# An encoder block in exact halves: eight seven-product columns instead of five, and low halves formed by an adding DMA queue

## The chip, the cores and the metric

The kernel runs on one core of a Trainium2 chip. The core has a matrix engine (TensorE, PE in the profile), a vector engine (VectorE, DVE), a scalar engine (ScalarE, ACT), a general engine (GpSimd, POOL) and a queue engine (SyncE, SP). Each runs its own list of instructions in order; they wait for one another by semaphores. PE reads its operands from SBUF, the on-chip memory of 128 partitions, and adds its products up in PSUM, eight banks of 128 x 512 float32; DVE and ACT read PSUM. DMA transfers are issued from SP, ACT or POOL and are carried by 16 DMA engines. The metric is the time of one execution in microseconds (us), measured on the device.

## What is computed

One layer of a residual block on x, 512 tokens by 1024 features, all in float32:

```python
h = rms_norm(x, g1)
x = x + (sigmoid(g_A) * y_A + sigmoid(g_B) * y_B) @ w_out      # two attention branches of h
x = x + conv_glu(rms_norm(x, g2))

def conv_glu(h):
    hid = h @ w_up                          # 1024 -> 2 * 2816
    hid = causal depthwise conv of width 3 along the tokens, + bias
    gate, up = hid[:, :2816], hid[:, 2816:]
    return (silu(gate) * up) @ w_down       # 2816 -> 1024
```

The change touches only conv_glu, the last 45% of the time.

## The kernel before

**Halves.** PE's fast format keeps only part of a float32. Each operand is therefore split: the high half is the value rounded to that format (a cast on ACT), the low half is the value minus the high half (a subtraction on DVE). A product is three matmuls: high x high, high x low, low x high (mm3, L251). Whatever is multiplied must first pass through ACT and DVE for this.

**Up-projection.** The 2 x 2816 columns of w_up are worked off as 22 column pairs, j = 0 to 21, each 128 gate columns and the 128 up columns that belong to them ("column j" below). A column's weights are 1 MB; SP loads them two columns ahead into two raw buffers, ACT and DVE split them one column ahead (split_gen, L204). A plain column (up_body, L935) is 2 x 8 products of 128 x 128 weights with 512 tokens: 48 matmuls of 512 columns. Columns 0 and 1 run interleaved with the end of the stage before.

A column in SEVEN (L63) is computed by seven block products instead of eight (up_seven, L986). Weights and the normed tokens are cut into 2 x 2 blocks (halves of the features; gate and up columns, or halves of the tokens), and by Winograd's form of Strassen's scheme seven products of blocks or of block sums give all four result blocks. This is 7 x 4 x 3 = 84 matmuls of 256 columns. It needs sums of token blocks (ts, four tiles, formed once at the start of the stage), sums of weight blocks (block_sums, L173, four DVE instructions, in the column pair before last) and halves of seven blocks instead of four (split_seven, L188), and the result blocks are put together by four copies on ACT and five additions on DVE (L1003 to L1024). Before, SEVEN is columns 5, 8, 11, 14 and 17.

After a column's products come the convolution (conv, L849: one ACT and two DVE instructions for the gate, the same for the up part), SiLU on ACT and the gating product on DVE (L928). The result u of column j lies in one of four slots of ub.

**Pairs.** The down-projection uses the seven-product scheme as well, on pairs of columns. When columns 2i and 2i+1 are done, pair_sums(i) forms the block sums (L898 to L901, in a tile st with one buffer, and in u itself) and the halves of seven operands: four go to a tile ax of 2048 columns, three to a tile ay of 1536 (L904 to L912; the first half of each tile holds the high halves, the second the low ones). The high half is written by ACT (L908), the low half by DVE (L909). For i = 0 to 8 this happens in the up-projection, pairs 9 and 10 are finished inside the down-projection.

**Down-projection.** Two passes over the 11 pairs. The first (s = 0) takes the four products that use ax, the second (s = 1) the three that use ay. A step of a pass, dn0_i or dn1_i, is 24 or 18 matmuls of 512 columns. Its weights come from SP into the same raw buffers and are split on ACT and DVE one step ahead (split_down, L139). Split n = 1 is placed behind the last column's convolution (L155 to L158).

**Where the operands lie.** ax0 to ax7 have eight buffers of the tag "ax"; ax8 takes a buffer of the token sums, whose last use is column 17. All ay up to pair 6 share one buffer: each is stored to DRAM (L933) on POOL's queue and fetched again (fetch, L948) into space that has come free. fetch 0 to 4 stand in the program behind column 18, 5 and 6 in the first pass (L1175). keep[0] is a place for weights that the second pass needs again.

**Order.** The program gives the instructions in the order of the code. The order in which each engine gets them is laid out at compile time by a list scheduler along a modelled timeline, so that an instruction that is ready by the model can be taken ahead of earlier ones that are not. In the profile the work on a pair runs up to 20 us behind the end of its columns, and fetches appear ahead of their place in the code.

Of the kernel before, what the change touches and what calls it, by code (L numbers as in the profile page):

```python
# [8 lines left out]
F32 = mybir.dt.float32  # L9
F32R = mybir.dt.float32r  # L10
AF = mybir.ActivationFunctionType
ALU = mybir.AluOpType
# [3 lines left out]
P = 128  # L16
S = 512
# [42 lines left out]

CHUNKS = _chunks()

SEVEN = (5, 8, 11, 14, 17)  # L63


@with_exitstack
def block_kernel(ctx: ExitStack, tc: tile.TileContext, x, xt, params, g2, rbx, wts, wd0, wd1, out):
    nc = tc.nc
    V, A, G, PE, SP = nc.vector, nc.scalar, nc.gpsimd, nc.tensor, nc.sync
# [41 lines left out]
    keep = {}  # L111
# [58 lines left out]
    def is_seven(i):  # L170
        return i < len(order) and order[i] in [f"up{j}" for j in SEVEN]

# [69 lines left out]
    def run_chunk(key, body, pieces=4):  # L242

        sp = split_gen(pos[key] + 1, pieces)
        for _ in body(*splits.pop(key)):
            next(sp, None)
            yield
        for _ in sp:
            pass
# [12 lines left out]
    pp = ctx.enter_context(tc.tile_pool(name="pp", bufs=1, space=PSUM))  # L262
    dram = ctx.enter_context(tc.tile_pool(name="dram", bufs=1, space=bass.MemoryType.DRAM))
    htd = dram.tile([NT, 2, P, S], F32, tag="htd", name="htd")
    ayd = dram.tile([7, P, 1536], F32, tag="ayd", name="ayd")


    reset = pool_c.tile([P, S], F32, tag="reset", name="reset")
# [560 lines left out]
    hi, lo = splits.pop("wo3")  # L829
# [8 lines left out]
    fp = late["pool"] = ctx.enter_context(tc.tile_pool(name="fp", bufs=1))  # L838
# [5 lines left out]
    pairs = {}  # L844
# [4 lines left out]
    def conv(ps, tile_idx, c):  # L849
        cw = lambda j: par[:, C_CW + 2 * NF * j + tile_idx:C_CW + 2 * NF * j + tile_idx + 1]  # L850
        tap = A.activation(c, ps, AF.Identity, scale=cw(2), bias=par[:, C_CB + tile_idx:C_CB + tile_idx + 1])
        late["tap"] = (tap,)
        V.scalar_tensor_tensor(c[:, 1:], ps[:, 0:S - 1], cw(1), c[:, 1:], op0=ALU.mult, op1=ALU.add)
        V.scalar_tensor_tensor(c[:, 2:], ps[:, 0:S - 2], cw(0), c[:, 2:], op0=ALU.mult, op1=ALU.add)
# [9 lines left out]
    def gate(j, pg):  # L864
        g = fp.tile([P, S], F32, tag="cg", name=f"cg{j}", bufs=1)
        conv(pg, j, g)
        A.activation(g, g, AF.Silu)
        return g

    def pair_sums(i):  # L870

        u0, u1 = ub[:, 2 * i % 4, :], ub[:, 2 * i % 4 + 1, :]
        u = ub[:, 2 * i % 4:2 * i % 4 + 2, :].rearrange("p a b -> p (a b)")
        lo_, hi_ = slice(0, 256), slice(256, 512)
        t = {}
        if i < 8:
            ax = fp.tile([P, 2048], F32R, tag="ax", name=f"ax{i}", bufs=8)
            ay = fp.tile([P, 1536], F32R, tag="ay", name=f"ay{i}")
        elif i == 8:

            ax = fp.tile([P, 2048], F32R, tag="ts", name=f"ax{i}", bufs=4)
            ay = fp.tile([P, 1600], F32R, tag="wxh", name=f"ay{i}")[:, 0:1536]
            keep[0] = fp.tile([P, S], F32, tag="hg", name="t2_0")
        else:

            ax = late["hp"].tile([P, 2048], F32R, tag=f"ax{i}", name=f"ax{i}")
            ay = late["hp"].tile([P, 1536], F32R, tag=f"ay{i}", name=f"ay{i}")
        pairs[i] = (ax, ay)

        def sums():  # L890
            t["st"] = st = fp.tile([P, 768], F32, tag="st", name=f"st{i}", bufs=1)
            s1, s42 = st[:, 0:256], st[:, 256:768]
            if i == 9:

                s42 = fp.tile([P, S], F32, tag="cg", name="s42_9", bufs=1)
            s4, s2 = s42[:, 0:256], s42[:, 256:512]
            t["s42"] = s42
            ins = [V.tensor_tensor(s1, u0[:, hi_], u1[:, hi_], op=ALU.add),  # L898
                   V.tensor_tensor(u0[:, hi_], u0[:, lo_], u0[:, hi_], op=ALU.subtract),
                   V.tensor_tensor(s2, s1, u0[:, lo_], op=ALU.subtract),  # L900
                   V.tensor_tensor(s4, u1[:, lo_], s2, op=ALU.subtract)]  # L901
            return ins

        def halves(a, parts):  # L904
            ins, n = [], a.shape[-1] // 2
            for o, src in parts:
                sl = slice(o, o + src.shape[-1])
                A.copy(a[:, sl], src)  # L908
                ins.append(V.tensor_tensor(a[:, n + o:n + sl.stop], src, a[:, sl].bitcast(F32), op=ALU.subtract))  # L909
            return ins  # L910
        return (sums, lambda: halves(ax, ((0, u[:, 0:768]), (768, t["st"][:, 0:256]))),
                lambda: halves(ay, ((0, u[:, 768:1024]), (256, t["s42"]))))  # L912

    def keep_place(i):
# [8 lines left out]
    def up_fin(j, pg, pu, g=None):  # L923
        if g is None:
            g = gate(j, pg)
        u = ub[:, j % 4, :]
        conv(pu, NF + j, u)
        late["fin"] = (V.tensor_tensor(u, g, u, op=ALU.mult),)  # L928
        if j % 2 == 1 and j // 2 < 9:
            for step in pair_sums(j // 2):  # L930
                step()
            if j // 2 < 7:
                G.dma_start(ayd[j // 2], pairs[j // 2][1].bitcast(F32))  # L933

    def up_body(j):  # L935
        def body(hi, lo):
            pg, pu = BANK(f"pg{j}", j - 1), BANK(f"pu{j}", j - 1)
            yield from up_mm(pg, hi, lo, 0, 0, S)
            g = gate(j, pg)
            if j in (2, 3):  # L940
                next(late["ts"])
            yield from up_mm(pu, hi, lo, P, 0, S)
            up_fin(j, pg, pu, g)
            if j in (2, 3):
                next(late["ts"])
        return body

    def fetch(i):  # L948

        tag = {0: "sx", 1: "wxl"}.get(i, "ts" if i < 5 else "ax")  # L950
        n, bufs = {"sx": (1536, 1), "wxl": (1600, 1), "ts": (2048, 4), "ax": (2048, 8)}[tag]
        ay = fp.tile([P, n], F32R, tag=tag, name=f"ay{i}", bufs=bufs)[:, 0:1536]
        G.dma_start(ay, ayd[i])
        pairs[i] = (pairs[i][0], ay)
# [3 lines left out]
    ts = {}  # L958
# [27 lines left out]
    def up_seven(j):  # L986
        def body(hi, lo, wh, wl):
# [35 lines left out]
            V.tensor_tensor(hu[:, left], b7, hu[:, right], op=ALU.add)  # L1023
            V.tensor_tensor(hu[:, right], hu[:, right], pc[:, 1], op=ALU.add)  # L1024
            up_fin(j, None, hu, g)
            yield
        return body
# [4 lines left out]
    def up_first(j):  # L1032
        def body(hi, lo):
            pg, pu = BANK(f"pg{j}", 0), BANK(f"pu{j}", 0)
            halves.append((hi, lo, pg, pu))
            yield from up_mm(pg, hi, lo, 0, 0, 256)
            yield from up_mm(pu, hi, lo, P, 0, 256)
            if j == 1:
                n = 0
                for i, (h, l, g, u) in enumerate(halves):  # L1040
                    for o, ps in ((0, g), (P, u)):
                        for _ in up_mm(ps, h, l, o, 256, S):
                            n += 1
                            if n == 1 or 4 <= n < 8:
                                next(late["ts"])
                            yield
                    up_fin(i, g, u)
        return body

    late["ts"] = token_sums()  # L1050
    for j in range(NF):
        body = up_first(j) if j < 2 else up_seven(j) if j in SEVEN else up_body(j)
        for _ in run_chunk(f"up{j}", body, pieces=4 if j < 2 else 2):
            pass
        if j == 18:
            for i in range(5):
                fetch(i)


# [48 lines left out]
    def late_pair(steps):  # L1108

        for step in steps:  # L1110
            for ins in step():
                chain("halves", ins)
            yield
# [34 lines left out]
    def down_body(s, i):  # L1148
        order_ = ((1, 2, 5, 7), (6, 3, 4))[s]

        def body(hi, lo):
            for n, p in enumerate(order_):
                product(s, p, i, hi, lo)
                if s == 0 and i == NP - 1:
                    fin0(p)
                if n == 2:
                    next(steps, None)
                yield
        return body
# [10 lines left out]
    def steps0():  # L1170
        yield
        for i in (9, 10):
            ss[i] = pair_sums(i)
            yield from late_pair(ss[i][:2])
            fetch(i - 4)  # L1175

    def steps1():
        tmp["x"] = [fp.tile([P, 2, D], F32, tag="ax", name=f"x_{r}", bufs=8) for r in range(2)]
# [7 lines left out]
    for s in range(2):  # L1186
        steps = (steps0, steps1)[s]()
        for i in range(NP - 2 * s):
            for _ in run_chunk(f"dn{s}_{i}", down_body(s, i), pieces=2):
                pass  # L1190

    for _ in split_gen(pos[f"dn1_{NP - 1}"], 2):
        pass
# [13 lines left out]
def _layout(inputs):  # L1207
# [12 lines left out]
    for i, (key, kn, parts) in enumerate(CHUNKS[:-2 * NP]):  # L1220
        views = [f[name][0][r0:r0 + kn * P, c0:c0 + n] for name, r0, c0, n in parts]
        w = views[0] if len(views) == 1 else np.concatenate(views, axis=1)
        if key in [f"up{j}" for j in SEVEN]:

# [26 lines left out]
```

## Time and profile before

| | us |
|---|---|
| median of 3 runs | 726.53 (726.07 to 726.63) |
| profiled execution | 726.66 |
| its span, first to last instruction | 724.9 |
| PE busy in the span | 718.6 (99%) |
| DVE busy | 565.4 (78%) |
| ACT busy | 401.5 (55%) |
| POOL busy | 53.6 (7%) |
| up-projection, column 2 to the first matmul of the down-projection | 402.8 to 615.6 |

The profile is of one execution. A row of a group of instructions gives the line of the code, the engine, the operation, out<-in by the program's names, the shape and count, then busy time in us and the mean of one in ns, then the idle time of the engine before them with what ended it. Rows of waits give total, count and longest. Rows of the timeline give start and duration. The instructions of an engine overlap a little, so durations add up to somewhat more than busy time.

### The profile page before, as it was taken

How to read it: one execution, taken by the hardware profiler on the slowest of the kernel's cores; microseconds unless marked ns; L12 is line 12 of the kernel's file. 1: busy time of each engine (PE TensorE's matmuls, PEld its weight loads, DVE VectorE, ACT ScalarE, POOL GpSimd, SP SyncE). 2: the span in 40 equal slices, each digit the busy share in tenths (PEclk: the TensorE clock that was granted, in tenths of full speed). 3: DMA queues.
4: the chain of work that ended last, by engine and by line, in shares of the span. 5: the costliest groups of instructions: out<-in, count | busy, mean ns of one | idle time of the engine just before them, and what ended most of it. 6: DMA issues, size and time to landing. Idle time of an engine off the chain costs nothing.

```text
span 724.9 us, 10589 instructions
## 1 busy us (share of the span) xinstructions
PE 718.6 (99%) x4019; PEld 627.5 (87%) x4019; DVE 565.4 (78%) x1030; ACT 401.5 (55%) x727; POOL 53.6 (7%) x95
## 2 busy tenths in 40 slices
PE   8999999999999999999999999999999999999997
PEld 8999998888988888888889889889898988888886
DVE  6678867775988888566275799998979985997686
ACT  6675656657767676442254556655545653543541
POOL 2701200000101011000012000000000100000000
PEclk9999999999999999999999999999999999999999
DMA  8632232211313111314536613544335553564563
GB/s 308 250 131 78 83 117 74 74 59 58 118 63 113 59 59 59 136 68 144 195 149 239 203 62 156 186 135 160 118 145 186 181 184 117 173 243 174 177 222 116
DMA packets 24786, 100.91 MB, mean 139 GB/s; under 512 B 2592, under 2 KB 7328, under 8 KB 17184
## 3 DMA queue, kind: packets, MB, share of 16 engines
q1 hardware_dynamic: 21792, 87.00, 33.8%
q0 software_dynamic: 2656, 13.11, 5.0%
q8 instruction: 31, 0.51, 0.3%
q14 instruction: 19, 0.16, 0.1%
q10 hardware_dynamic: 288, 0.14, 0.1%
HBM read 88.44 MB, written 11.80 MB: 138 GB/s over the span
## 4 chain that ended last, share of the span: by engine, by line
PE 98%; DMA 1%; SPq 0%; DVE 0%; ACT 0%; DVEq 0%; issue 0%
PE P L1087 14%; PE p L998 7%; PE pg L254 4%; PE pg L253 4%; PE pg L255 4%; PE pu L254 4%; PE pu L255 4%; PE pu L253 4%; PE qkB L255 2%; PE gB L255 2%; PE qkB L253 2%; PE gA L253 2%; PE gA L254 2%; PE gB L253 2%; PE gA L255 2%; PE qkB L254 2%
## 5 line engine op out<-in xcount | busy, mean ns | idle before, releaser
L253 PE MATMUL pg<-hth,whi_up 128*128 128x512 f32 (+1 forms) x152 | 55.7, 367 | 0.0
L255 PE MATMUL pg<-hth,wlo_up 128*128 128x512 f32 (+1 forms) x152 | 55.7, 366 | 0.0
L254 PE MATMUL pg<-htl,whi_up 128*128 128x512 f32 (+1 forms) x152 | 55.7, 366 | 0.0
L254 PE MATMUL pu<-htl,whi_up 128*128 128x512 f32 (+1 forms) x152 | 55.6, 366 | 0.0
L253 PE MATMUL pu<-hth,whi_up 128*128 128x512 f32 (+1 forms) x152 | 55.6, 366 | 0.0
L255 PE MATMUL pu<-hth,wlo_up 128*128 128x512 f32 (+1 forms) x152 | 55.6, 365 | 0.0
L1087 PE MATMUL P<-whi_dn,ax 128*128 128x512 f32 x176 | 54.4, 389 | 0.0
L149 ACT CAST whi_dn<-raw_dn 128x1024 fp32r<-128x1024 f32 x33 | 34.3, 1051 | 25.5 <-PE P L1087 15.2
L145 DVE TENSOR_TENSOR wlo_dn<-raw_dn,whi_dn 128x1024 fp32r<-128x1024 f32 x33 | 40.0, 1224 | 9.2 <-ACT whi_dn L149 9.1
L228 DVE TENSOR_TENSOR wlo_up<-raw_up,whi_up 128x1024 fp32r<-128x1024 f32 (+1 forms) x40 | 41.2, 1062 | 7.0 <-ACT whi_up L226 7.0
L226 ACT CAST whi_up<-raw_up 128x1024 fp32r<-128x1024 f32 (+1 forms) x40 | 34.5, 917 | 14.7 <-PE pu L254 7.9
L1087 PE MATMUL P<-whi_dn,ay 128*128 128x512 f32 x132 | 40.8, 389 | 0.0
L1087 PEld LDWEIGHTS P<-whi_dn,ax 128*128 128x128 f32 x176 | 33.0, 188 | 6.8
L1087 PE MATMUL P<-wlo_dn,ax 128*128 128x512 f32 x88 | 34.2, 389 | 0.0
L254 PEld LDWEIGHTS pu<-htl,whi_up 128*128 128x128 f32 x152 | 28.6, 188 | 4.7
L253 PEld LDWEIGHTS pu<-hth,whi_up 128*128 128x128 f32 x152 | 28.5, 188 | 4.7
L255 PEld LDWEIGHTS pg<-hth,wlo_up 128*128 128x128 f32 x152 | 28.6, 188 | 4.7
L255 PEld LDWEIGHTS pu<-hth,wlo_up 128*128 128x128 f32 x152 | 28.5, 188 | 4.6
L253 PEld LDWEIGHTS pg<-hth,whi_up 128*128 128x128 f32 x152 | 28.6, 188 | 4.6
L254 PEld LDWEIGHTS pg<-htl,whi_up 128*128 128x128 f32 x152 | 28.6, 188 | 4.5
L633 DVE TENSOR_TENSOR_SCAN aB<-aB,reset 128x127 f32<-128x127 f32 (+3 forms) x32 | 26.0, 817 | 6.7 <-ACT aB L628 6.7
L1087 PEld LDWEIGHTS P<-whi_dn,ay 128*128 128x128 f32 x132 | 24.8, 188 | 5.1
(303 smaller groups left out, 2240.3 us busy)
## 6 DMA issues: line engine op xcount, KB each, us to landing
raw_up<-in_wts SPq DMA_DIRECT2D x22, 1024.0 KB, 4.8
raw_dn<-in_wd SPq DMA_DIRECT2D x11, 1024.0 KB, 4.8
raw_dn<-in_wd SPq DMA_DIRECT2D x11, 512.0 KB, 3.4
ayd<-ay POOLq DMA_DIRECT2D x7, 768.0 KB, 5.2
ay<-ayd POOLq DMA_DIRECT2D x7, 768.0 KB, 6.5
raw_gA<-in_wts SPq DMA_DIRECT2D x4, 1024.0 KB, 4.7
raw_qkB<-in_wts SPq DMA_DIRECT2D x4, 1024.0 KB, 4.8
raw_gB<-in_wts SPq DMA_DIRECT2D x4, 1024.0 KB, 4.7
```

Source lines behind the costliest of these rows:

```text
L145: chain("halves", V.tensor_tensor(o, x, y, op=op))
L149: chain("casts", A.copy(hi[:, sl], src))
L226: A.copy(hi[:, sl], raw[:, sl])
L228: E.tensor_tensor(lo[:, sl], raw[:, sl], hi[:, sl].bitcast(F32), op=ALU.subtract)
L253: PE.matmul(ps, sh, mh, start=first, stop=False)
L254: PE.matmul(ps, sh, ml, start=False, stop=False)
L255: PE.matmul(ps, sl, mh, start=False, stop=last)
L633: V.tensor_tensor_scan(ar, ar, reset[:, S - n:S - 1][:, ::-1], 1.0, op0=ALU.mult, op1=ALU.max)
L998: PE.matmul(ps, st, mv[:, k, :], start=first and k == 0 and n == 0, stop=last and k == 3 and n == 2, skip_group_check=True)
L1087: chain("products", PE.matmul(dst, st, mv, start=first and n == 0, stop=last and n == 2, skip_group_check=True))
```

## The change

Eight columns instead of five are computed by seven products; from column 8 on it is every second one.

The low halves of pairs 0 to 8 are no longer formed by DVE. ACT writes the negative of the rounded value into the low half's place, and a DMA on POOL's queue, which adds to its destination, adds the value itself from SBUF. Pairs 9 and 10 keep the subtraction on DVE.

As column 20 is now a seven, the token sums and the buffers of the block sums are in use until then. ax8 therefore takes a ninth turn of the eight "ax" buffers, in the place of ax0: ax0 is stored to DRAM after pair 6 (axd) and fetched into a buffer of the token sums after column 20, beside keep[0], which moves from pair 8 to the same place. ay of pair 7 is stored and fetched as well. Only fetches 0 and 1 stand behind column 20; the others are spread over the steps of the down-projection.

```diff
-SEVEN = (5, 8, 11, 14, 17)
+SEVEN = (5, 8, 10, 12, 14, 16, 18, 20)
...
-    ayd = dram.tile([7, P, 1536], F32, tag="ayd", name="ayd")
+    ayd = dram.tile([8, P, 1536], F32, tag="ayd", name="ayd")
+    axd = dram.tile([P, 2048], F32, tag="axd", name="axd")
...
-        if i < 8:
+        if i < 9:
             ax = fp.tile([P, 2048], F32R, tag="ax", name=f"ax{i}", bufs=8)
             ay = fp.tile([P, 1536], F32R, tag="ay", name=f"ay{i}")
-        elif i == 8:
-
-            ax = fp.tile([P, 2048], F32R, tag="ts", name=f"ax{i}", bufs=4)
-            ay = fp.tile([P, 1600], F32R, tag="wxh", name=f"ay{i}")[:, 0:1536]
-            keep[0] = fp.tile([P, S], F32, tag="hg", name="t2_0")
...
                 sl = slice(o, o + src.shape[-1])
+                lo = a[:, n + o:n + sl.stop]
                 A.copy(a[:, sl], src)
-                ins.append(V.tensor_tensor(a[:, n + o:n + sl.stop], src, a[:, sl].bitcast(F32), op=ALU.subtract))
+                if i < 9:
+
+                    A.activation(lo, src, AF.Copy, scale=-1.0)
+                    G.dma_start(lo, src, accum_op=ALU.add)
+                else:
+                    ins.append(V.tensor_tensor(lo, src, a[:, sl].bitcast(F32), op=ALU.subtract))
             return ins
...
-            if j // 2 < 7:
+            if j // 2 < 8:
                 G.dma_start(ayd[j // 2], pairs[j // 2][1].bitcast(F32))
+            if j // 2 == 6:
+
+                G.dma_start(axd, pairs[0][0].bitcast(F32))
...
-        tag = {0: "sx", 1: "wxl"}.get(i, "ts" if i < 5 else "ax")
-        n, bufs = {"sx": (1536, 1), "wxl": (1600, 1), "ts": (2048, 4), "ax": (2048, 8)}[tag]
+        tag = {0: "sx", 1: "wxl", 2: "wxh"}.get(i, "ts" if i < 6 else "ax")
+        n, bufs = {"sx": (1536, 1), "wxl": (1600, 1), "wxh": (1600, 1), "ts": (2048, 4), "ax": (2048, 8)}[tag]
...
-        if j == 18:
-            for i in range(5):
+        if j == SEVEN[-1]:
+            keep[0] = fp.tile([P, S], F32, tag="hg", name="t2_0")
+            ax0 = fp.tile([P, 2048], F32R, tag="ts", name="ax0_", bufs=4)
+            G.dma_start(ax0, axd)
+            pairs[0] = (ax0, None)
+            for i in range(2):
                 fetch(i)
...
             yield from late_pair(ss[i][:2])
-            fetch(i - 4)
...
             for _ in run_chunk(f"dn{s}_{i}", down_body(s, i), pieces=2):
                 pass
+            n = ({1: 2, 3: 6, 5: 7, 7: 3, 9: 4}, {0: 5})[s].get(i)
+            if n is not None:
+                fetch(n)
```

## The prediction

> **What bounds the kernel now.** I read the page first: busy shares, then the chain of waits.
>
> ```profile
> span 724.9 us, 10589 instructions
> PE 718.6 (99%) x4019; PEld 627.5 (87%) x4019; DVE 565.4 (78%) x1030; ACT 401.5 (55%) x727; POOL 53.6 (7%) x95
> PE 98%; DMA 1%; SPq 0%; DVE 0%; ACT 0%; DVEq 0%; issue 0%
> ```
>
> TensorE (PE) is busy 99% of the span, and 98% of the chain that ended last is its own work. A busy share alone would not prove that it is fed, so the next view is what PE waited for in the whole span:
>
> ```profile
> PE warm L301 <- DVE warm L298: 1.1, 1, 1.1
> PE qA L379 <- ACT whi_qA L226: 0.6, 1, 0.6
> PE qA L379 <- DVE whi_qA L224: 0.4, 1, 0.4
> ```
>
> All three lie in the first microseconds. From the up-projection on PE waits for nothing. So time is saved here only by fewer PE cycles, and lost only if something begins to starve PE. The third view is the timeline of PE at the column borders: a seven-product column (5), two plain ones (6, 7), and the start of the next seven (8).
>
> ```profile
> 435.44 0.28 PE L998 MATMUL p<-hth,whi_up 128*128 128x256 f32 x1
> 445.33 0.40 PE L253 MATMUL pg<-hth,whi_up 128*128 128x512 f32 x1
> 456.24 0.39 PE L253 MATMUL pg<-hth,whi_up 128*128 128x512 f32 x1
> 467.12 0.28 PE L998 MATMUL p<-hth,whi_up 128*128 128x256 f32 x1
> ```
>
> A seven costs 445.33 - 435.44 = 9.89 us (84 matmuls, 117.7 ns apart), a plain column behind it 10.91, a plain column behind a plain one 10.88 (48 matmuls, 226.7 ns apart).
>
> The fourth view is the busy time of the engines in stretches of three columns (no seven; one seven) and in the two last columns, 20 and 21:
>
> ```profile
> 402.77:435.44 32.67, 32.67 (x147) 27.04 (x146) 29.38 (x38) 17.73 (x23) 0.00 (x0) 1.00 0.36 120
> 498.80:530.47 31.67, 31.67 (x181) 27.92 (x180) 28.65 (x45) 18.57 (x30) 1.07 (x2) 1.00 0.35 125
> 593.86:615.62 21.76, 21.76 (x97) 18.02 (x96) 13.64 (x17) 8.16 (x10) 0.00 (x0) 1.00 0.27 97
> ```
>
> Columns after the length: PE, PEld, VectorE (DVE), ScalarE (ACT), GpSimd (POOL), granted clock, DMA share, GB/s. The clock is 1.00 throughout. DVE is the engine next to its limit: 28.65 of 31.67 us (90%).
>
> **The change, part by part.**
>
> *Three more sevens* (eight columns instead of five, from column 8 on every second one). Each is followed by a plain column, so a seven and its follower take 9.89 + 10.91 = 20.80 us, against 2 x 10.88 = 21.76 for two plain ones: 0.96 each. Three of them: **-2.88 us**. This is certain as far as PE stays fed.
>
> The Trainium skill, "TensorE: Matmul & The Clock Gate", section "Back-to-back issue gap", puts a warm matmul of N columns at N/2.4 + 2.5 ns: 215.8 ns for 512 and 109.2 for 256. By that a plain column would be 10.36 us, a seven 9.17, and three sevens would save 3.57. The rows above (226.7 and 117.7 ns) disagree with it in this kernel, and I keep theirs.
>
> *What the sevens ask of DVE, and what the adding queue takes from it.* Groups of DVE between 402.77 and 615.62, shapes kept apart:
>
> ```profile
> L228 DVE TENSOR_TENSOR wlo_up<-raw_up,whi_up 128x1024 fp32r<-128x1024 f32 x28 | 33.6, 1222 | 4.0 <-ACT whi_up L226 4.0
> L928 DVE TENSOR_TENSOR ub<-cg,ub 128x512 f32<-128x512 f32 x21 | 14.5, 691 | 2.5 <-ACT cg L867 2.1
> L853 DVE SCALAR_TENSOR_TENSOR cg<-pg,par,cg 128x511 f32<-128x511 f32 x16 | 12.0, 748 | 3.2 <-ACT cg L851 3.2
> L909 DVE TENSOR_TENSOR ax<-ub,ax 128x768 fp32r<-128x768 f32 x9 | 8.6, 955 | 0.0
> L909 DVE TENSOR_TENSOR ay<-st,ay 128x512 fp32r<-128x512 f32 x9 | 6.2, 689 | 0.0
> L909 DVE TENSOR_TENSOR ay<-ub,ay 128x256 fp32r<-128x256 f32 x9 | 3.8, 424 | 0.0
> L898 DVE TENSOR_TENSOR st<-ub 128x256 f32<-128x256 f32 x9 | 3.8, 423 | 0.1
> L909 DVE TENSOR_TENSOR ax<-st,ax 128x256 fp32r<-128x256 f32 x9 | 3.8, 421 | 0.0
> ```
>
> The low halves of a pair (L909) cost 0.955 + 0.689 + 0.424 + 0.421 = 2.49 us of DVE; they leave DVE for nine pairs. A plain column is four convolution steps of 0.748, one product of 0.691 and two low halves of 1.222: 6.13. A seven adds four block sums and one low half more of 0.69, one of 1.222 and five evacuations of 0.42: 6.13 + 3.45 + 1.22 + 2.12 = 12.92. The sums of a pair are four of 0.423: 1.69. Check on the stretch with one seven: 12.92 + 2 x 6.13 + 1.5 x (2.49 + 1.69) = 31.45 of durations, where the window shows 28.65 busy; neighbouring instructions overlap, factor 0.91. With the change a seven, a plain column and one pair without low halves: (12.92 + 6.13 + 1.69) x 0.91 = **18.9 us of DVE in 20.80 (91%)**, against 90% now. Had the low halves stayed on DVE, it would be 18.9 + 2.27 = 21.2, more than the 20.80 of PE: the cover that makes the sevens free is this removal. So I cost the extra DVE work at 0, with 1.9 us of room per two columns.
>
> How early the operands are ready is the other half of the cover. DVE's last low half for column 9, and in the down-projection the low halves of its second block row (dn0_1) and one that waits for its weights:
>
> ```profile
> 468.57 2.37 DVE L228 TENSOR_TENSOR wlo_up<-raw_up,whi_up 128x1024 fp32r<-128x1024 f32 x2
> 618.82 2.36 DVE L145 TENSOR_TENSOR wlo_dn<-raw_dn,whi_dn 128x1024 fp32r<-128x1024 f32 x2
> 653.96 1.42 DVE L145 TENSOR_TENSOR raw_dn<-raw_dn 128x512 f32<-128x512 f32 x2 [0.60 <-DMA raw_dn<-in_wd]
> ```
>
> The first ends at 470.94, and column 9 starts some 6 us later, when the seven that began at 467.12 has taken its 9.89. In the up-projection DVE may thus be about 6 us late before PE stops, and the convolutions and pair sums can slip further still. In the down-projection the lead is small: its first block row starts at 615.62 (end of the last window above), takes 24 matmuls x 0.2267 = 5.44, so dn0_1 starts at 621.06, and the first half of its operand is ready at 618.82 + 1.2 = 620.0: 1 us.
>
> *ACT* takes over two things: three more sevens and, per pair, a second write of each part (minus the rounded value).
>
> ```profile
> L908 ACT CAST ax<-ub 128x768 fp32r<-128x768 f32 x9 | 7.5, 834 | 3.6 <-DVE ub L899 3.6
> L908 ACT CAST ay<-st 128x512 fp32r<-128x512 f32 x9 | 5.6, 620 | 5.7 <-DVE st L901 5.7
> L908 ACT CAST ay<-ub 128x256 fp32r<-128x256 f32 x9 | 3.7, 406 | 11.0 <-DVE ub L928 11.0
> L908 ACT CAST ax<-st 128x256 fp32r<-128x256 f32 x9 | 3.6, 401 | 3.8 <-DVE st L898 3.8
> ```
>
> The second write is not in the trace; its nearest rows are these, 2.26 us a pair, and it could at most be twice that. Two columns now: 18.57 less one plain column (8.16 / 2 = 4.08) = 14.5 with 1.5 pairs; with one pair written twice 14.5 + 0.5 x 2.26 = 15.6 of 20.80 (75%), at the upper bound 17.9. Nothing for PE: 0.
>
> *The adding queue.* 36 transfers of 128 to 384 KB from SBUF to SBUF on POOL's queue. No row shows one that adds; the nearest:
>
> ```profile
> raw_dn<-in_wd SPq DMA_DIRECT2D x11, 1024.0 KB, 4.8
> ayd<-ay POOLq DMA_DIRECT2D x7, 768.0 KB, 5.2
> ay<-ayd POOLq DMA_DIRECT2D x7, 768.0 KB, 6.5
> htd<-xf_n POOLq DMA_DIRECT2D x8, 256.0 KB, 3.3
> ```
>
> Below: 3.3 us each and overlapping. Above: 6.5 each, one after the other, 26 a pair. I take about 4, partly overlapping, since the sizes sit nearer the 256 KB row. Queued behind them on POOL is only the store of ay, which must now wait for its two adds; waiting on them is the next pair's write of the sums tile (one buffer), a period of 20.80 us later, and of the u tiles two periods later. Below 20.80 they cost 0.
>
> The Trainium skill, "DMA: Bandwidth & Descriptors", section "Anatomy of one DMA", fits a transfer of this queue by 2.0 us + bytes / 436 GB/s; as an estimate from that page an add of 384 KB would be 2.9 us and four in series under 10. The trace's 256 and 768 KB rows (3.3 and 5.2) are above that fit (2.6 and 3.8), and no run so far shows an add.
>
> *The detour of ax0 and the fetches.* One store of 1 MB in column 13, one load of 1 MB back and eight fetches of 768 KB instead of seven. Where POOL issues fetches now:
>
> ```profile
> 553.31 0.55 POOL L953 DMA_DIRECT2D ay<-ayd  x1 [23.25 <-DVE wxl_up L200]
> 627.07 0.53 POOL L953 DMA_DIRECT2D ay<-ayd  x1 [48.24 <-PE P L1087]
> ```
>
> They go out as soon as their buffer is free, also ahead of their place in the program. ax0 comes back into the slot that the second product of column 20 frees: with column 20 starting near 615.62 - 2.88 - 10.91 - 9.89 = 591.9, that is 594.7; by the ay row (6.5, at most twice that) it lands by 601 to 608, before the down-projection starts at 612.7. It is hidden: 0; without that cover PE would wait what is over. Fetched ay parts are needed only in the second pass, some 60 us later. At the end of column 21 DVE is 13.64 of 21.76 busy now, and gets five evacuations (2.1) more: 0.
>
> **Sum.** Profiled execution: span 724.9, its own time 726.66, so 1.8 lies around the span. 726.66 - 2.88 = 723.8. The median of the runs, 726.53, is 0.13 below the profiled one: **723.7**.
>
> **The rivals.** *A, forecast:* PE stays fed, 723.7 (723.1 to 724.9: the 0.5 us spread of the runs, and one or two short stalls).
>
> *B, DVE becomes the bound of the alternating columns.* For it: 91% in a queue that runs in order, not all of its room is usable; the stretches of one seven show 83 to 100%. Against: no stall at 90% now, 6 us of lead. If DVE could be filled to 85% only, two columns take 18.9 / 0.85 = 22.2, and the sevens would be slower than plain; at 90%, 21.0, a loss of 0.2 x 6 periods = 1.2: 724.9. At 88%, 21.5: loss 4, over the whole stretch limited by the lead of 6 us and the lighter columns 20 and 21, so about 2: 725.9. I take 725.7, no measurable change.
>
> *C, slower: the fetches meet the weights in the first down pass.* Fetches 6 and 7 wait for ax2 and ax3; 3, 4 and 5 stand behind them, so POOL could issue four at one time near 635. A weight load of 1 MB then shares the 16 engines with 3 MB. At 1 MB per 4.8 us each fetch pushes it by up to 3.6; four of them 14. The room is the 1 to 2 us of lead and about 2 us between landing and use. It decides from a push of 4 us; at half of the 14, 3 are lost; with the whole, 10: 726.7 to 733. I take 730. For it: the 0.60 us that DVE already waits for weights at 653.96. Against: two fetches in this stretch cost nothing now, and those with free slots may go out before the down-projection.
>
> *D, the adding queue is too slow.* If four adds and the store are served in series, 4 x 6.5 + 5.2 = 31 a pair, over 20.80 by 10; the sums then wait, DVE's queue stops behind them, and PE after 6 us: for seven pairs some 60 us, near 785. It decides from 20.80 a pair. Against: three fetches issued together now land without blocking POOL.
>
> **How the numbers follow.** A 0.64, B 0.16, C 0.13, D 0.07. What can be told from no change is about 0.2%, 1.45 us: faster is below 725.1, slower above 728.0. A and a quarter of B are faster: 0.68. The rest of B and 0.03 of C are the same: 0.15. Slower: 0.17. Range: from 723.0 (A's lower end) to 728.0, which takes in B and the mild part of C.
>
> **What would show it.** A right: PE waits still only at the start, p L998 x672 at the same 9.89 a column, eight of them; the first down-projection matmul near 612.7; L909 only for pairs 9 and 10. B: PE idle in front of matmuls of whi/wlo/wxl, released by DVE L200 or L228, in columns 9 to 20. C: DVE L145 or PE L1087 waiting for raw_dn. D: DVE L898 or ACT L851 released by an adding transfer. The forecast is wrong if columns 2 to 21, now 615.62 - 402.77 = 212.85 us, still take over 211.4.

## The result: slower, and the profile after

The changed kernel takes 762.85 us (median of 4 runs, 755.51 to 765.73), the kernel before 726.3 on the same chip: ratio 1.0488, 95% interval 1.0412 to 1.0565. The forecast was 723.7, at most 728.0. The profiled execution took 765.73. Four later executions, of 1108 to 2570 us, are left out of the ratios below; two of them were the profiled ones, so the run with five sevens and 1024 bytes and the one with the adds of ay alone have no trace to read.

Line numbers from here on are those of the kernel after, also in the experiments: the sums of a pair L894 to L897, a part's high half L905, the negative of it L908, the add L909, the store of ay L935, the fetches L958, the products of a seven L1003, their copies out of PSUM L1008 to L1021, the down-projection L1096.

From the page of the kernel after, the span and PE's busy time:

```profile
span 764.0 us, 10995 instructions
PE 730.8 (96%) x4127; PEld 639.7 (84%) x4127; DVE 566.3 (74%) x1027; ACT 424.2 (56%) x781; POOL 87.3 (11%) x135
```

Then windows of the same kernel (after the length: PE, PEld, DVE, ACT, POOL, granted clock, DMA share, GB/s): the plain columns 2 to 4; the seven of column 5 with 6 and 7; six periods of a seven and a plain column (8 to 19); columns 20 and 21; the down-projection.

```profile
403.28:435.94 32.66, 32.66 (x146) 27.04 (x145) 29.21 (x37) 20.17 (x27) 2.64 (x3) 1.00 0.43 126
435.94:473.26 37.32, 33.69 (x182) 29.52 (x181) 24.98 (x39) 19.66 (x32) 6.81 (x9) 0.95 0.67 194
473.26:622.60 149.34, 132.73 (x794) 118.80 (x792) 110.51 (x173) 84.57 (x143) 24.39 (x31) 0.95 0.56 154
622.60:650.46 27.86, 24.49 (x133) 21.94 (x133) 22.33 (x33) 15.12 (x24) 5.96 (x10) 0.88 0.88 272
650.46:759.83 109.37, 106.60 (x463) 86.02 (x461) 89.43 (x116) 46.53 (x58) 1.10 (x3) 1.00 0.55 195
```

And the down-projection of the kernel before:

```profile
615.62:720.71 105.09, 105.09 (x463) 86.47 (x461) 88.52 (x114) 45.90 (x57) 1.07 (x2) 1.00 0.51 182
```

The plain columns cost what they did. The six periods take 149.34 / 6 = 24.9 us each, where 20.80 was forecast. Column 2 to the end of the up-projection is 650.46 - 403.28 = 247.18, before it was 212.85: +34.3. The down-projection adds 109.37 - 105.09 = 4.3, the start 0.5. That is the whole difference of the spans, 39.1.

Against the forecast for the up-projection, 212.85 - 2.88 = 209.97, the loss is 37.2. PE is busy for 33.69 + 132.73 + 24.49 of the three lower stretches and for 32.66 of the first, 223.57 in all. So 247.18 - 223.57 = 23.6 us are idle, and 223.57 - 209.97 = 13.6 are the same work taking longer, at a lower granted clock (0.95, 0.95, 0.88). What PE waited for:

```profile
PE p L1003 <- ACT pc L1008: 16.9, 7, 3.7
PE p L1003 <- DVE wlo_up L200: 2.7, 3, 1.2
PE P L1096 <- DVE wlo_dn L145: 2.6, 3, 1.0
PE p L1003 <- ACT whi_up L199: 2.2, 2, 1.7
PE pg L253 <- DVE hu L1018: 1.7, 1, 1.7
```

Seven times, inside the sevens, PE stops for up to 3.7 us until ACT has copied a product out of PSUM. The Trainium skill, "TensorE: Matmul & The Clock Gate", section "Part 1: The HAM clock gate", says that the clock halves after an idle window of about 3.4 us. The longest pauses here are of that length: after the 3.48 us before 583.17 the clock granted from 585.0 to 586.5 was 0.50. But the 1.92 us before 443.68 were enough as well:

```profile
444.00:447.00 3.00, 3.00 (x15) 3.00 (x15) 1.22 (x3) 0.95 (x2) 0.05 (x1) 0.50 1.01 408
```

After the pauses of 1.28 and 1.37 us (before 531.31 and 509.11) the clock stayed at 1.00.

ACT was not overloaded (56% busy), nor was DVE: in the six periods they work 84.57 / 6 = 14.1 and 110.51 / 6 = 18.4 us a period, where 15.6 and 18.9 were forecast. ACT was late because it waited itself. Three rows from the waits of all engines; in the kernel before, none of these instructions waits for a DMA:

```profile
ACT ay L905 <- DMA ayd<-ay: 39.9, 6, 10.2
...
POOL ayd L935 <- DMA ay<-st: 20.2, 4, 6.6
...
DVE st L894 <- DMA ay<-st: 17.9, 4, 5.3
```

How they hang together is seen in the timeline around one pair (start, duration, engine, line; rows of several engines put in order of time):

```profile
565.76 0.42 DVE L894 TENSOR_TENSOR st<-ub 128x256 f32<-128x256 f32 x1 [3.67 <-DMA ay<-st]
566.25 0.56 POOL L935 DMA_DIRECT2D ayd<-ay  x1 [6.82 <-issue]
569.90 0.41 ACT L905 CAST ay<-ub 128x256 fp32r<-128x256 f32 x1 [7.71 <-DMA ayd<-ay]
571.03 0.85 POOL L909 DMA_DIRECT2D ay<-ub  x1 [4.22 <-ACT ay L908]
574.00 0.85 POOL L909 DMA_DIRECT2D ax<-st  x1 [2.12 <-ACT whi_up L199]
575.73 0.63 ACT L908 ACTIVATE ay<-st 128x512 fp32r<-128x512 f32 x1
576.94 0.84 POOL L909 DMA_DIRECT2D ax<-ub  x1 [2.08 <-ACT ay L908]
583.17 0.39 PE L1003 MATMUL p<-hth,whi_up 128*128 128x256 f32 x1 [3.48 <-ACT pc L1008]
583.63 0.86 POOL L909 DMA_DIRECT2D ay<-st  x1 [5.84 <-ACT pc L1008]
587.27 0.56 POOL L935 DMA_DIRECT2D ayd<-ay  x1 [2.78 <-DMA ay<-st]
```

ACT finished the last part's second write at 576.36, but its add went out at 583.63. In between POOL did nothing: the add ahead of it was under way. The DMA issues of the stretch give the landing of that one:

```profile
ax<-ub POOLq DMA_DIRECT2D x1, 384.0 KB, 6.4
```

576.94 + 6.4 = 583.3, and 0.3 us later the next add is issued. The releasers in brackets on POOL's rows are inferred and miss this. So the adds are served one at a time. From the first add of a pair to the landing of the store it is 587.27 + 6.3 - 571.03 = 22.5 us here, and 25.3 for the pair before (544.45 to 569.8): more than the 20.80 of two columns. And the next pair can't begin earlier, since ay has one buffer: at 569.90 ACT's first write into ay has waited 7.71 us for the store of the previous pair to land. So the loop of write, adds and store sets the pace: the first adds of five successive pairs went out at 519.68, 544.45, 571.03, 594.82 and 621.31, 25.4 us apart on average. ACT works in order, so the splits and PSUM copies behind that write are late; DVE stands likewise, 3.67 us, in front of st.

### The profile page after: what moved, and what is told of

It reads as the page before. It is cut to its first block, busy times and chain, and to the rows that moved or that the text cites. A ratio compares the mean times of both kernels' runs of the same rounds, so it can differ in the third digit from the quotient of the medians.

```text
span 764.0 us, 10995 instructions
## 1 busy us (share of the span) xinstructions
PE 730.8 (96%) x4127; PEld 639.7 (84%) x4127; DVE 566.3 (74%) x1027; ACT 424.2 (56%) x781; POOL 87.3 (11%) x135
## 2 busy tenths in 40 slices
DMA packets 30549, 112.87 MB, mean 148 GB/s; under 512 B 3232, under 2 KB 10272, under 8 KB 22688
## 3 DMA queue, kind: packets, MB, share of 16 engines
q0 software_dynamic: 8416, 25.04, 12.3%
## 5 line engine op out<-in xcount | busy, mean ns | idle before, releaser
L1096 PE MATMUL P<-whi_dn,ax 128*128 128x512 f32 x160 | 49.7, 391 | 0.0
L149 ACT CAST whi_dn<-raw_dn 128x1024 fp32r<-128x1024 f32 x33 | 34.1, 1049 | 27.4 <-DMA raw_dn<-in_wd 14.6
L253 PE MATMUL pg<-hth,whi_up 128*128 128x512 f32 (+1 forms) x128 | 46.5, 364 | 1.7 <-DVE hu L1018 1.7
L254 PE MATMUL pg<-htl,whi_up 128*128 128x512 f32 (+1 forms) x128 | 46.4, 362 | 0.0
L255 PE MATMUL pg<-hth,wlo_up 128*128 128x512 f32 (+1 forms) x128 | 46.3, 362 | 0.0
L254 PE MATMUL pu<-htl,whi_up 128*128 128x512 f32 (+1 forms) x128 | 46.3, 362 | 0.0
L253 PE MATMUL pu<-hth,whi_up 128*128 128x512 f32 (+1 forms) x128 | 46.3, 362 | 0.0
L255 PE MATMUL pu<-hth,wlo_up 128*128 128x512 f32 (+1 forms) x128 | 46.2, 361 | 0.0
L1096 PE MATMUL P<-whi_dn,ay 128*128 128x512 f32 x132 | 40.8, 389 | 0.0
L1003 PE MATMUL p<-hth,whi_up 128*128 128x256 f32 x64 | 21.2, 331 | 19.1 <-ACT pc L1008 16.9
L228 DVE TENSOR_TENSOR wlo_up<-raw_up,whi_up 128x1024 fp32r<-128x1024 f32 (+1 forms) x34 | 34.0, 1029 | 3.0 <-ACT whi_up L226 3.0
L1096 PEld LDWEIGHTS P<-whi_dn,ax 128*128 128x128 f32 x160 | 30.0, 188 | 6.4 <-ACT whi_dn L149 0.3
L1096 PE MATMUL P<-wlo_dn,ax 128*128 128x512 f32 x80 | 31.7, 396 | 2.7 <-DVE wlo_dn L145 2.6
L1003 PEld LDWEIGHTS p<-hth,whi_up 128*128 128x128 f32 x64 | 14.0, 219 | 21.9 <-ACT pc L1008 18.3
L905 ACT CAST ay<-ub 128x256 fp32r<-128x256 f32 x11 | 4.5, 406 | 47.4 <-DMA ayd<-ay 39.9
L636 POOL TENSOR_SCALAR_AFFINE_SELECT bB<-bB 128x128 f32<-128x128 f32 x32 | 13.6, 427 | 149.2 <-DVE bB L635 139.7
L1096 PEld LDWEIGHTS P<-whi_dn,ay 128*128 128x128 f32 x132 | 24.8, 188 | 5.1
```

The source lines that it names most:

```text
L149: chain("casts", A.copy(hi[:, sl], src))
L228: E.tensor_tensor(lo[:, sl], raw[:, sl], hi[:, sl].bitcast(F32), op=ALU.subtract)
L253: PE.matmul(ps, sh, mh, start=first, stop=False)
L254: PE.matmul(ps, sh, ml, start=False, stop=False)
L255: PE.matmul(ps, sl, mh, start=False, stop=last)
L636: G.affine_select(b[:, n - P:n], b[:, n - P:n], pattern=[[-1, P]], compare_op=ALU.is_gt, fill=0.0, base=0, channel_multiplier=1)
```

## The experiments

Theory S: with the 512 bytes of descriptor space that the kernel gives POOL's queue, only one add fits at a time; the pair's chain of adds and store is longer than two columns, and ay and st hand the delay to ACT and DVE. Rival O: eight alternating sevens ask too much of ACT and DVE, whoever forms the low halves. Rival C of the prediction (fetches against weights) stays in reserve for the down-projection. Ratios below are to the kernel before, with 95% intervals.

**More descriptor space.** Order and number of instructions are the same on every engine.

```diff
-dynamic_dma_scratch_size=512
+dynamic_dma_scratch_size=1024
```

> The changed kernel, and the only edit is the space of the queue's descriptors in SBUF, 1024 instead of 512 bytes per partition; the instructions and their order on every engine are the same. Theory S (the queue takes one adding transfer at a time because its descriptor space holds only one, and the four adds and the store of a pair then need about 25 us in series, over the 20.8 us that PE needs for two columns): adds follow one another by about 1 us where their data is ready, PE no longer waits for the copies at L1008, and the time falls to 723 to 735. Rival Q (an adding transfer is not begun before the one ahead has landed, whatever the space): unchanged, 755 to 766, adds still 3 to 7 us apart. Rival O (the order in which ACT and DVE are given their work with alternating sevens starves PE): unchanged too, but with adds close together.

Measured 735.64 (730.87 to 741.84), ratio 1.0155 (1.0100 to 1.0209). One number gives back 27 of the 36.5 us. Adds are now issued 0.4 us after ACT's write and overlap; in one place a fourth waited, with three under way (ready at 465.86, issued at 470.41). S holds for three quarters of the loss; 9 us stay, so the time is just above the range that S gave.

**No adds.** All low halves on DVE again, eight sevens and everything else as after.

```diff
-                if i < 9:
+                if i < 0:
```

> The changed kernel with the low halves of all pairs on VectorE, as before the change; eight sevens, the detour of ax0 and the new places of the fetches stay. Theory S: without adds nothing is in series; VectorE would need 21.2 us per two columns against 20.8 of PE, so 0 to 3 us of waits: 724 to 728. Rival O: the alternating sevens starve PE by themselves: 740 or more.

Measured 729.57 (728.47 to 731.71), ratio 1.0044 (1.0029 to 1.0060): 1.6 us above what S gave, far from what O gave. The only wait of PE from column 2 on in its profiled execution, the slowest of the five:

```profile
PE P L1096 <- DVE cg L855: 2.8, 1, 2.8
```

PE runs through all eight sevens: the up-projection takes 615.99 - 405.59 = 210.4 us, one early matmul of the down-projection included. DVE's backlog shows only at the start of the down-projection, where PE waits 2.8 us for a bank that the last convolution has not drained. O is no explanation for 36 us. It is what rival B of the prediction describes, here with the low halves on DVE, and the wait is of the size of B's price (about 2).

**The adds with five sevens.**

```diff
-SEVEN = (5, 8, 10, 12, 14, 16, 18, 20)
+SEVEN = (5, 8, 11, 14, 17)
```

> The changed kernel with the five seven-product columns of before (5, 8, 11, 14, 17); the adding queue, the detour of ax0 and the fetches stay. Theory S: PE now takes 21.1 us per pair, the series of adds some 25, so it stays clearly slower than before: 735 to 755. Rival O: 726 to 729, since the columns are as before.

Measured 761.6 (760.59 to 763.22), ratio 1.0486 (1.0470 to 1.0501): as slow as with eight, and above the range of either theory.

```profile
PE pg L253 <- ACT whi_up L226: 13.8, 4, 5.8
PE pg L253 <- DVE hu L1018: 3.3, 1, 3.3
```

Here PE waits mostly for ACT's weight casts, which stand behind the same late write of ay. With 512 bytes the adds alone cost about 35 us; the three more sevens have no part in it.

**Five sevens and 1024 bytes** (both edits above).

> The run with five sevens and all adds, now with 1024 bytes of descriptor space; order of all engines as in that run (761.6). If the series of adds was its whole cost, it comes back to the time of the kernel before, 726 to 729. If adds that are no longer in series still cost something by themselves (ACT's second write, transfers beside the weight loads, waits of VectorE for the sums tile), it stays above, 730 to 740.

Measured 728.8 (727.1 to 729.3), ratio 1.0033 (1.0020 to 1.0045), against 761.6 with 512 bytes: 33 of the 35 us are the descriptor space. Beside five sevens the four adds cost 2.4 us with 1024 bytes, beside eight 9: of what stays, the sevens do have a part.

**Two adds a pair, 512 bytes**: those of ax only.

```diff
-                if i < 9:
+                if i < 9 and a is ax:
```

> The changed kernel with adds only for the two parts of ax; the two parts of ay get their low halves on VectorE. Theory S: two adds and a store that waits for neither, about 3 + 5 + 5 = 13 us a pair on the queue, under 20.8; VectorE 18.9 + 1.0 = 19.9 us: 723.5 to 728. Rival Q and theory S agree here; rival O: 740 or more.

Measured 730.97 (729.61 to 733.0), ratio 1.0064 (1.0045 to 1.0083), 3 us above the expected range. The timeline of POOL:

```profile
530.68 0.84 POOL L909 DMA_DIRECT2D ax<-st  x1 [16.41 <-DVE wlo_up L200]
538.67 0.86 POOL L909 DMA_DIRECT2D ax<-ub  x1 [7.15 <-ACT pc L1011]
539.57 0.56 POOL L935 DMA_DIRECT2D ayd<-ay  x1
```

The first add landed after 7.7 us, at 538.4, and only then the second went out (ACT had its data ready at 533.6). The store of ay, a plain transfer, follows at once, while that second add is under way. So it is an add behind an add that waits. Two in series are far shorter than two columns; of the loss about 5 us are left, and PE waits 4.7 us in the up-projection.

**One add a pair, 512 bytes**: ax from ub, the largest.

```diff
-                if i < 9:
+                if i < 9 and src.shape[-1] == 768:
```

> The changed kernel, 512 bytes, with one add per pair only (the 768-column part of ax); the other three parts get their low halves on VectorE. One add has nothing of its kind to queue behind, so the small space should not matter; VectorE 18.9 + 1.4 = 20.3 of 20.8 us. Expected 724 to 729. If a single add per pair still costs 5 us or more (732 and up), it is not the series.

Measured 726.78 (724.88 to 728.45), ratio 1.0003 (0.9993 to 1.0012). In its trace, the fastest of its runs, PE waits for nothing from column 2 on, and the up-projection takes

```profile
403.00:613.22 210.22, 210.22 (x1251) 187.39 (x1250) 195.57 (x307) 131.56 (x198) 16.53 (x25) 1.00 0.55 181
```

210.22 us, 2.63 less than before. That execution is 1.9 us shorter than the one before (spans 723.0 and 724.9). So the gain of the three sevens is real where PE is fed, but the median of the runs does not show it; the nine slower runs, 725.76 to 728.45, have no trace.

**Seven sevens without adds** (the last seven in column 18).

```diff
-SEVEN = (5, 8, 10, 12, 14, 16, 18, 20)
+SEVEN = (5, 8, 10, 12, 14, 16, 18)
...
-                if i < 9:
+                if i < 0:
```

> No adds, sevens 5, 8, 10, 12, 14, 16, 18: column 20 is plain again. In the run without adds PE was fed through all eight sevens and then waited 2.8 us at the start of the down-projection for a bank that VectorE had not drained. If that is VectorE's backlog from 21.2 us of work per 20.8, two light columns at the end take it away: -1.9 us for two more sevens than before, 724 to 726. If the wait has another cause, 728 or more.

Measured 725.78 (725.5 to 727.12), ratio 0.9995 (0.9985 to 1.0004): no measurable change. DVE's backlog of the kernel with eight is gone without any add, and in the trace the up-projection takes 210.95 us, 1.90 less than before, which is two sevens at 0.96.

**Which adds cost the rest, with 1024 bytes.** The two of ax, the two of ay, the one of ay from st (`a is ax`, `a is ay`, or also a width of 512 in the condition):

> Adds for both parts of ax, 1024 bytes of descriptor space; order as in the run with adds for ax alone (731.0). There the second add began only when the first had landed, and PE waited about 5 us in columns 9 to 15 for banks that VectorE drained late. If that lateness comes from the adds: 724 to 728. If it comes from VectorE's load (19.9 of 20.8): 730 to 732, unchanged.

> Eight sevens and the larger descriptor space (1024 bytes), adds only for the two parts of ay; ax keeps DVE's subtraction. It asks what the 9 us are that are left of the loss once the adds overlap (735.6 with all four adds, 727.2 with the two of ax). Theory L, the loop through the single ay buffer (the high-half copy of the next pair waits on ACT for the store of ay, the store for ay's adds): nearly all of the 9 us are here, 733 to 736, with ACT L905 waiting for ayd. Theory T, the number of adds and second writes, whichever tile they go to: half of it, near 727 to 730, and no wait of ACT for ayd that PE feels.

> Eight sevens, 1024 bytes, one add a pair: ay from st, 256 KB, the last part of a pair and the one that the store of ay waits for; 0.69 us of DVE a pair are saved. Theory L: the add is still the last link ahead of the store, so part of the wait for ayd stays, 729 to 732. Theory T: one add a pair is harmless like the one of ax from ub (726.8 measured), 725 to 727.

Measured: ax 727.23, ratio 1.0008 (0.9994 to 1.0022); ay 725.48, ratio 0.9993 (0.9984 to 1.0002); ay from st alone 727.4, ratio 1.0013 (1.0002 to 1.0023). I had expected one of the first two to carry most of the 9 us, or each a half. Neither carries a part that can be measured: theory L (the loop through the single ay buffer) falls, and T (each add has its price) as well. Nearly all of the rest comes only when the four adds and the eight sevens are together (three adds, below, cost 2 us).

**The add for late pairs only; the add with seven sevens.**

```diff
-                if i < 9:
+                if 5 <= i < 9 and src.shape[-1] == 768:
```

> Eight sevens, 512 bytes, one add (ax from ub, 384 KB) for pairs 5 to 8 only; the rest on DVE. Without any add DVE was behind at the start of the down-projection and PE waited 2.8 us there (729.6); with this add for all nine pairs 726.8 was measured, with 724.9 in the profiled execution. If it is the late backlog that has to be relieved, four adds of 0.83 us of DVE each suffice: 725 to 726.5. If DVE's backlog builds up from column 8 on, it stays near 728 to 729.5.

> Seven sevens (to column 18), 512 bytes, one add a pair (ax from ub). Without adds the same columns gave 725.8 with no wait of PE. If an add of 384 KB a pair costs nothing by itself: 725.5 to 726. If its traffic on the 16 engines delays weights or operands a little in each pair: 726.5 to 727.5.

Measured 730.57, ratio 1.0055 (1.0043 to 1.0068), and 726.01, ratio 1.0005 (0.9995 to 1.0014). The first is a miss, above both ranges, for the guess that relief late is enough: PE waits 3.1 us at the start of the down-projection, as without any add. The second is seven sevens again, neither better nor worse.

**Is it the adding?** The 36 transfers as plain copies, with 512 and with 1024 bytes, and three adds a pair (without ax from ub) with 1024.

```diff
-                    G.dma_start(lo, src, accum_op=ALU.add)
+                    G.dma_start(lo.bitcast(F32), src)
```

> The changed kernel with its 36 adding transfers turned into plain copies of the same parts to the same places (the low halves then hold the value itself, so the result is not the block's; the order and number of instructions on every engine are the same). If the descriptor space of 512 bytes holds only one transfer of this kind whatever it does: the copies go out one after another like the adds, 755 to 765. If only adding takes so much (two descriptors where a copy has one, or a wait for the destination): copies overlap and the time is near the one with 1024 bytes, 725 to 736.

> The same copies with 1024 bytes. If the 9 us that four adds a pair lose with 1024 bytes come from the adding itself (the destination is read as well, long landings that delay the weights): 725 to 728. If they come from the number of transfers and of second writes on ACT, which are the same here: 732 to 737.

> 1024 bytes, three adds a pair (ax from ub, the largest, stays a subtraction on DVE). If the loss grows with the traffic beside the weight loads, most of it goes with the largest add, 726 to 729. If it is the fourth transfer that finds no place and waits for a landing, as some do in the trace with four, also 726 to 729, but then no add waits for a landing here. If it is the loop through the single ay buffer, which is unchanged here, 732 to 737.

Measured: copies with 512 bytes 727.44, ratio 1.0022 (1.0003 to 1.0040); copies with 1024 bytes 727.19, ratio 1.0008 (0.9995 to 1.0020); three adds with 1024 bytes 728.45, ratio 1.0028 (1.0013 to 1.0043). The timeline of POOL with copies and 512 bytes:

```profile
563.84 0.54 POOL L909 DMA_DIRECT2D ay<-ub  x1 [10.28 <-DVE hu L1028]
565.17 0.54 POOL L909 DMA_DIRECT2D ax<-st  x1 [0.79 <-ACT ax L908]
568.81 0.55 POOL L909 DMA_DIRECT2D ax<-ub  x1 [3.10 <-DVE cg L854]
570.48 0.54 POOL L909 DMA_DIRECT2D ay<-st  x1 [1.13 <-DVE cg L855]
575.98 0.54 POOL L935 DMA_DIRECT2D ayd<-ay  x1 [4.96 <-DMA ay<-st]
```

The same transfers, the same space, the same bytes: ax from ub goes out at 568.81 and takes 5.8 us to land, and ay from st follows at 570.48 without waiting for it. The copies differ from the adds in one thing more, they are declared to write float32 and not the fast format. That is not the reason: the fetches write float32 into tiles of the fast format without adding, and in the kernel before, with the same 512 bytes, three of them go out one behind the other in 1.6 us, while the four between 560 and 600 us landed after 7.7 us at the median:

```profile
572.82 1.61 POOL L953 DMA_DIRECT2D ay<-ayd  x3 [18.37 <-PE p L998]
```

```profile
ay<-ayd POOLq DMA_DIRECT2D x4, 768.0 KB, 7.7
```

Of the transfers tried, only those that add stand in line behind their like. What an add takes up in the 512 bytes stays open. The packets of POOL's queue seem to tell, without adds, with 36 copies, with 36 adds (packets, MB, share of the DMA engines' time):

```profile
q0 software_dynamic: 3232, 16.78, 6.0%
```

```profile
q0 software_dynamic: 5536, 25.04, 9.1%
```

```profile
q0 software_dynamic: 8416, 25.04, 12.3%
```

A copy is (5536 - 3232) / 36 = 64 packets, an add (8416 - 3232) / 36 = 144, the same for the nine adds of 384 KB alone. But one fetch alone, in a window of the kernel before, has 144 as well:

```profile
q0 software_dynamic: 144, 0.79, 34.9%
```

So three plain transfers of 144 packets were under way in the space that held one add of 144: the number of packets does not explain it. How many bytes of the space an add takes was not measured.

**The rest with 1024 bytes.** In the profiled execution of the first experiment, the fastest of its runs, the up-projection takes 215.91 us, 5.7 more than the 210.22 above; PE is idle for 3.7 of it:

```profile
403.04:618.95 215.91, 212.18 (x1251) 189.06 (x1249) 185.31 (x278) 139.65 (x225) 39.70 (x52) 0.99 0.69 201
```

One of the two pauses, in its timeline:

```profile
545.26 0.85 POOL L909 DMA_DIRECT2D ax<-st  x1 [0.48 <-DVE st L896]
548.62 0.85 POOL L909 DMA_DIRECT2D ax<-ub  x1 [2.51 <-ACT ax L908]
549.68 0.84 POOL L909 DMA_DIRECT2D ay<-st  x1 [0.22 <-issue]
557.80 0.69 DVE L179 TENSOR_TENSOR sx_up<-raw_up 128x512 f32<-128x512 f32 x1 [3.46 <-DMA raw_up<-in_wts]
558.41 0.74 DVE L855 SCALAR_TENSOR_TENSOR cg<-pg,par,cg 128x510 f32<-128x510 f32 x1
559.25 0.63 ACT L868 ACTIVATE cg<-cg 128x512 f32<-128x512 f32 x1 [2.86 <-DVE cg L855]
560.19 0.38 PE L1003 MATMUL p<-hth,wxh_up 128*128 128x256 f32 x1 [2.11 <-ACT pc L1011]
```

Two adds run beside a load of weights. DVE waits 3.46 us for it, with a convolution step (L855) queued behind; ACT's SiLU waits for that step, the PSUM copy stands behind the SiLU, and PE waits for the copy. L179 is a block sum, which only a seven has; that fits the smaller price beside five sevens. The loads between 435 and 590 us (median time to landing at the end of the row), before and then with four adds and 1024 bytes:

```profile
raw_up<-in_wts SPq DMA_DIRECT2D x14, 1024.0 KB, 4.9
```

```profile
raw_up<-in_wts SPq DMA_DIRECT2D x14, 1024.0 KB, 6.1
```

With 1024 bytes and the two adds of ax the same figure is 4.8, with four copies 5.3, with three adds 5.3. The time follows it only roughly: by the ratios and medians 0.6, 0.6, 2 and 9 us over before. So the chain from a late load to PE is shown for these pauses, and the lateness grows with overlapping adds. That this is all of the 9 us is not shown: the profiled run was the fastest (730.87 of 730.87 to 741.84), and no slower one has a trace.

## Why the prediction was wrong

**The adding queue** is the term that failed. It was costed at 0, by "about 4, partly overlapping"; the single landings were well estimated (medians of 2.7 to 4.7 us for 128 to 384 KB), the overlap was not. The adds are in series, and a pair took 22.5 and 25.3 us where two columns give 20.80. The estimate of four in series as under 10 us (its own terms add up to 10.1) was too low too: the four medians add up to 14.9. This is rival D at a smaller price: it forecast 31 a pair and a time near 785, "decides from 20.80 a pair", and its sign is in the trace, DVE in front of the sums of a pair, released by an adding transfer (17.9 us). With the measured 24.9 a period it is six times 4.1 = 24.6 us for columns 8 to 19, and the rest comes from the stretches at both ends. D had a chance of 0.07 because of "three fetches issued together now land without blocking POOL". Those were plain transfers, and the copies show that plain ones do overlap in that space. The evidence was sound, and about another kind of transfer.

**Who waits for the adds** was listed incompletely: the sums tile a period later, the u tiles two periods later. The first and worst waiter was missed: the single ay buffer, which ACT's high halves of the next pair need, and which is free only when the last add and then the store have landed. The front of this document names that buffer; the prediction did not follow it. That this link is the first and worst is read from the trace (39.9 us of ACT's time against 17.9 of DVE's); two buffers for ay were not tried. Behind ACT's write everything that ACT does for PE was late, and the lead of 6 us was gone at the first seven already (column 5 to 7: 37.32 us for 31.7).

**The clock** had no term. A bit over a third of the loss in the up-projection, 13.6 of 37.2 us, is PE running slower after its pauses.

**The three sevens, -2.88**: right in PE's time, 2.63 in the trace where PE is fed. In the medians of the runs the gain did not appear in any version; 725.5 to 727 is the best. Part of it goes at the start, in code that the change does not touch. Column 2 begins at 402.77 before; in three traces (without adds, four copies with 1024 bytes, seven sevens with one add) it begins at 404.76 to 405.59, and there the clock granted in the first 20 us is 0.91, where the kernel before has 1.00. PE's waits at its first weights (qA), 1.0 us in all before, are 1.8 to 2.4 in these three. Why the start is slower is open, and so is where the rest goes.

**DVE (rival B)**: the removal of the low halves was called the cover of the sevens. Without it PE is fed through all eight (210.4 us), and the price is the wait of 2.8 us behind them; of the 5.1 us by which that execution is longer than before, 2.8 lie ahead of column 2. Seven sevens cost nothing. So the cover was needed for the last seven only. That the 6 us of lead and the lighter columns at the end carry the others, as B's working had it, fits this and was not tried by itself.

**ACT's second writes**: 0.842 us and 0.627 against the rows of 0.834 and 0.620 taken; right.

**The detour of ax0 and the fetches (rival C)**: with eight sevens and few adds the down-projection is within 0.5 us of before (105.55 after the one add a pair). So C did not happen by itself. In the kernel after, the down-projection lost 4.3 us, 2.6 of them in waits for low halves of its weights; its 1 MB loads took 6.9 us at the median, 4.8 before, and ACT's casts waited 14.6 us for them, 2.5 before. That late fetches ran into those loads there is likely and was not tried by itself. The store of ax0 went out at 442.60, in column 5, not in column 13 as the prediction had it; nothing hung on that.

## What to carry to other kernels

A DMA that adds is not a copy that happens to add: here, in a small descriptor space, adds ran one at a time where copies and fetches overlapped. Evidence on overlap must come from transfers of the same kind, and the space is the first thing to raise. When work is moved from an engine to a queue, follow each tile it writes to its next writer, and set the latency of the whole chain, in series, against the period, not its bandwidth.

## What the runs showed of the hardware

- With 512 bytes an add whose data is ready is issued about 0.3 us after the previous one landed; with 1024 it is 0.4 us after its data is ready, and one that found three under way waited for a landing (issued at 470.41). Plain transfers overlap in 512 bytes, fetches of 144 packets too. Issuing one occupies POOL for 0.85 us, a copy for 0.54.
- An add of 128 KB from SBUF to SBUF (ay from ub) landed after 2.7 us at the median, a copy after 2.0; beside a load of weights single adds took 6.0 to 7.7 us.
- A pause of PE of 1.92 us was followed by a granted clock of 0.50, pauses of 1.28 and 1.37 us by 1.00.
- With four overlapping adds a pair a 1 MB load took 6.1 us at the median, with two of them 4.8, without 4.9: the price of contention is not proportional.
